# Ten of the 22 k rows of an FFN down projection by Strassen's seven products

## The chip, the cores and the metric

The kernel runs on one core of a Trainium2 chip. The metric is the device time of one execution in microseconds (us); the time given is the median of several runs. A profile of one further execution shows what each engine did: TensorE (PE, its weight loads apart as PEld), VectorE (DVE), ScalarE (ACT), GpSimd (POOL), and SyncE (SP), whose queue issues all the transfers here.

## The reference

Two layers of a bidirectional encoder on 512 tokens of width 1024. Each layer has four mixers (two kinds of attention over heads, a pooling mixer, and a latent attention), an output projection with a residual and a LayerNorm, and then a gated MLP with a short convolution. The change is in the last step of the MLP, the product with `w_down` (2816 x 1024):

```python
def _conv_ffn(x, w_up, conv_w, conv_b, w_down):
    u = x @ w_up
    u = lax.conv_general_dilated(u, conv_w[:, None, :], ...) + conv_b
    gate, up = jnp.split(u, 2, axis=-1)
    return (jax.nn.silu(gate) * up) @ w_down

def reference(...):
    for l in range(DEPTH):
        ...
        f = _conv_ffn(x, ffn_w_up[l], ffn_conv_w[l], ffn_conv_b[l], ffn_w_down[l])
        x = _layer_norm(DN_ALPHA * x + f, ln2_g[l], ln2_b[l])
    return x
```

## The kernel before

All matrix products are made in split precision: an operand x is held as hi = x rounded to the matmul's format and lo = x - hi, and a product is three matmuls, hi hi, hi lo and lo hi, summed in one PSUM bank (`mm3`). `hi_lo` makes the two parts: ACT casts (hi), then DVE subtracts (lo).

The kernel writes its instructions in an order that a planner chooses when the program is built. Each piece of work is a generator that says what it needs next (data, a free buffer, a PSUM bank); the planner follows expected times and gives every engine its fixed queue. On the chip each engine runs its queue in order and waits on semaphores. Two processes feed the weights: `p_raw` loads a group of weights (128 partitions x 1024 float32, 512 KB) through SP into a buffer of the pool "B" (34 buffers of 4 KB per partition), up to `DEPTH_RAW` = 4 groups ahead, and `p_split` makes hi and lo of it, up to `W.ahead` groups ahead of the group that TensorE uses.

A layer's MLP has two stages. In the up projection (`up_mm`), for each of 22 chunks of 128 channels (a "k row" of the next product), TensorE makes a gate half and an up half, 24 matmuls of 512 columns each; `up_post` adds the convolution (one ACT instruction, two on DVE), applies silu, multiplies gate and up on DVE, and splits the result into the tile G[j] (hi and lo, 128 x 512 each).

The down projection then has 22 k rows x 4 token tiles of 128 x 2 halves of 512 output columns. It is two calls of `gemm`. The first makes columns 0 to 511: 11 groups of two k rows, for each group 4 token tiles x 2 k rows x 3 matmuls into 4 PSUM banks, which hold the sums to the end of the call. `p_half` then adds each bank to the row of the residual (x times ALPHA) and takes statistics. The second call makes columns 512 to 1023 in the same way, with its last four groups done token tile by token tile (`tail`), so that the LayerNorm (`p_norm`) of one tile runs under the matmuls of the next.

Of the kernel before, what the change touches and what calls it, by code (L numbers as in the profile page):

```python
# [17 lines left out]
D = 1024  # L18
# [17 lines left out]
TAIL = 4  # L36
# [7 lines left out]
NB_E = 11  # L44
P_FIN, P_PREP, P_PV, P_T, P_S, P_G = 2, 1, 3, 4, 5, 9

# [52 lines left out]
    # -- memory  # L99
# [17 lines left out]
    # -- time  # L117
# [31 lines left out]
    # -- engines  # L149
# [71 lines left out]
    # -- processes  # L221
# [71 lines left out]
def trunk(ctx: ExitStack, tc: tile.TileContext, x_nat, x_t, pos, freqs, ident_d, bias_d, edge_d, ones_d,  # L293
# [35 lines left out]
    def hi_lo(hi, lo, src, scale=None, done=None):  # L329
        """steps: hi = f32r(src * scale), lo = src * scale - hi"""  # L330
# [18 lines left out]
    # ---------------- weights: loads run ahead, then raw -> (hi, lo)  # L349
    plan = []  # L350
    for l in range(DEPTH):
        plan += [(w_d[l, g], 832) for g in range(4)]
        plan += [(w_ab[l, c, g], 1024) for c in range(3) for g in range(4)]
        plan += [(w_c[l, c], 1024) for c in range(2)]
        plan += [(w_out[l, h, g], 1024) for h in range(2) for g in range(4)]
        plan += [(w_up[l, s * NCH + j], 1024) for j in range(NCH) for s in range(2)]
        plan += [(w_down[l, h, g], 1024) for h in range(2) for g in range(NCH // 2)]

    class W:
        raw, hl = {}, {}  # L360
        split, used, ahead, reserve, hold = 0, 0, AHEAD, RESERVE, False

    def p_raw():
        for n, (src, w) in enumerate(plan):
# [7 lines left out]
            P.dma(r[:, :w], src)  # L372
            W.raw[n] = r

    def p_split():
        for n, (src, w) in enumerate(plan):
            if n == 0:
                continue
            yield "if", lambda: n <= W.used + (min(URGENT, W.ahead) if W.hold else W.ahead) and n in W.raw
            yield "slot", "B", 2, lambda: max(0, W.reserve - 2)  # L380
# [17 lines left out]
    def drop(n):  # L398
        P.release(*W.hl.pop(n))

    # ---------------- constants
# [28 lines left out]
    def load_x(n):  # L430
        """the rows 256 n to 256 n + 256 of x^T, and before the second of them the first weights"""
# [157 lines left out]
    def gemm512(evac):  # L589
        """512 columns, some token tiles at a time"""  # L590
# [49 lines left out]
    def p_half(key, t, ps, cs, early=False):  # L640
        """x * alpha + ps for some columns of a row, and their statistics; early: a first part of ps alone"""
# [3 lines left out]
        if n < 512:  # L645
# [63 lines left out]
    def p_end(row, mv, rs, g, b, dst):  # L709
        """the last rows, in pieces: the output leaves as they are done"""  # L710
# [25 lines left out]
    # ---------------- one layer  # L736
    def layer(l, xkey):
# [32 lines left out]
        # ---- evacuations  # L770
# [16 lines left out]
        def evac_v(t, ps):  # L787
            """the values of A and of B"""
# [13 lines left out]
        def done_with(key):  # L802
            """one of the two that use the natural queries and keys is through with them"""
# [4 lines left out]
        # ---- D  # L808
# [89 lines left out]
        # ---- C  # L898
# [60 lines left out]
        # ---- queries and keys of a head  # L959
# [24 lines left out]
        def p_split_a(u):  # L984
            """[h h l] of the negated and scaled queries and [h l h] of the keys, side by side"""
# [29 lines left out]
        def stack_q(ps, dst, _, tok):  # L1015
            """a head's hi rows where they stand, its lo rows on the other 64 partitions"""
# [9 lines left out]
        def stack_k(ps, dst, kl, tok):  # L1026
            """a head's hi rows twice, and its lo rows twice"""
# [15 lines left out]
        def p_prep(kind, h):  # L1043
            u, h2 = h // 2, h % 2
            if kind == "B" and h2:
                QK[kind, h] = QK[kind, h - 1]
# [36 lines left out]
        # ---- attention  # L1083
# [171 lines left out]
        # ---- the stream of GEMMs  # L1255
        def stream():
# [40 lines left out]
            # gated MLP  # L1297
            G = [None] * NCH

# [17 lines left out]
            def up_post(j, side, keep):  # L1317
# [16 lines left out]
                yield "op", [(l, "silu", j), t1]  # L1334
                P.tt(t1, keep["t", 0], t1, ALU.mult)
# [21 lines left out]
            x2 = out if last else dr.tile([128, NT, D], F32, name=f"x2_{l}")  # L1357

            def LG(k):
                if k == NCH - 4:  # L1360
                    prog[0] = max(prog[0], 1)
                return G[k][:, 0], G[k][:, 1]

            def needg(k, t):
                return [(l, "G", k)]

            nk2 = (l, "x2")
            yield from gemm(512, LG, NCH, needg, lambda t, ps: P.spawn(p_half(k2, t, ps, slice(0, 512))))

            def after(g):  # L1370
                P.release(G[2 * g], G[2 * g + 1])
                if g >= 2:
                    prog[0] = 2
                if g >= 4:
                    W.ahead = 4

            yield from gemm(512, LG, NCH, needg, lambda *a: p_rest(k2, nk2, x2, last, *a), tail=TAIL, halve=True,
                            after=after)
            P.release(*G[-2 * TAIL:])
# [115 lines left out]
```

## Time and profile before

| | |
|---|---|
| median of 3 runs | 1224.42 us (1224.24 to 1224.9) |
| profiled execution, from first to last instruction | 1223.1 us (the page gives no other time of it) |
| TensorE busy | 1205.0 us, 6132 matmuls |
| VectorE busy | 804.0 us, 1305 instructions |
| ScalarE busy | 587.5 us, 1032 instructions |
| moved by DMA | 122.24 MB |

Busy times are sums over the span, and the stages differ much from one another. TensorE's clock is shown as the share granted: 1.00 is 2.4 GHz, 0.5 is 1.2 GHz.

### The profile page before, as it was taken

What the parts mean: (1) busy time and instruction counts of PE and PEld (TensorE: products, weight loads), DVE (VectorE), ACT (ScalarE), POOL (GpSimd) and SP (SyncE); (2) the same over time, 40 slices, a digit from 0 to 9 for tenths busy, and PEclk for the clock granted to TensorE, in tenths of its full rate; (3) what the DMA queues carried; (4) which work ended last, traced back from release to release, by engine and by line L of the source; (5) the groups of instructions that cost most, each with busy time, mean ns of one, the idle gap of its engine ahead of it and who ended that gap; (6) DMA issues with size and microseconds to landing.
All of it is one profiled execution on the core that took longest, in us unless ns stands there. A gap on an engine that the chain in (4) does not pass through costs nothing.

```text
span 1223.1 us, 16077 instructions
## 1 busy us (share of the span) xinstructions
PE 1205.0 (99%) x6132; PEld 1023.1 (84%) x6132; DVE 804.0 (66%) x1305; ACT 587.5 (48%) x1032; POOL 130.5 (11%) x247
## 2 busy tenths in 40 slices
PE   8999999999999999999999999999999999999997
PEld 7888888898888888888898888888988888888885
DVE  6678899875666666314656799989666666662325
ACT  6678787243444444212256878862444444441120
POOL 1320152100000000000131303501000000000002
PEclk9999999999999999999999999999999999999998
DMA  8112113371322222236351121234522322213431
GB/s 304 61 36 70 56 36 130 114 253 55 104 70 85 86 69 69 86 121 215 106 169 36 35 70 57 79 112 155 173 85 71 103 72 84 69 54 110 137 130 69
DMA packets 36221, 122.24 MB, mean 100 GB/s; under 512 B 5168, under 2 KB 6448, under 8 KB 36144
## 3 DMA queue, kind: packets, MB, share of 16 engines
q1 hardware_dynamic: 36144, 121.22, 30.5%
q8 instruction: 48, 0.79, 0.3%
q14 instruction: 29, 0.24, 0.1%
HBM read 112.81 MB, written 8.39 MB: 99 GB/s over the span
## 4 chain that ended last, share of the span: by engine, by line
PE 95%; DVE 3%; ACT 1%; issue 1%; POOL 0%; DMA 0%; POOLq 0%; DVEq 0%; ACTq 0%
PE ps_f L203 39%; PE g L203 29%; PE h L203 10%; PE ps_s L203 4%; PE ps_o L203 4%; PE ps_p L211 3%; PE ps_u L203 2%; PE ps_t L211 1%; PE ps_x L211 1%; PE ps_q L203 1%; PE ps_kv L203 0%; DVE m L199 0%; PE ps_r L211 0%; DVE lo L175 0%; DVE ptl L175 0%
## 5 line engine op out<-in xcount | busy, mean ns | idle before, releaser
L175 DVE TENSOR_TENSOR lo<-raw,hi 128x1024 fp32r<-128x1024 f32 (+2 forms) x185 | 223.8, 1218 | 179.0 <-ACT hi L167 156.4
L203 PE MATMUL ps_f<-xh,hi 128*128 128x512 f32 (+1 forms) x768 | 285.5, 372 | 0.0
L203 PE MATMUL ps_f<-xl,hi 128*128 128x512 f32 (+1 forms) x768 | 285.2, 371 | 0.0
L203 PE MATMUL ps_f<-xh,lo 128*128 128x512 f32 (+1 forms) x768 | 285.2, 371 | 0.0
L167 ACT CAST hi<-raw 128x1024 fp32r<-128x1024 f32 (+2 forms) x185 | 189.2, 1036 | 140.2 <-PE g L203 113.1
L203 PE MATMUL g<-hi,G 128*128 128x512 f32 (+1 forms) x712 | 217.9, 387 | 0.0
L183 DVE SCALAR_TENSOR_TENSOR t<-ps_f,cw,t 128x511 f32<-128x511 f32 x176 | 132.0, 750 | 74.7 <-ACT t L169 71.5
L203 PEld LDWEIGHTS ps_f<-xl,hi 128*128 128x128 f32 x768 | 144.7, 188 | 25.0
L203 PEld LDWEIGHTS ps_f<-xh,lo 128*128 128x128 f32 x768 | 144.6, 188 | 24.9
L203 PEld LDWEIGHTS ps_f<-xh,hi 128*128 128x128 f32 x768 | 144.7, 188 | 24.8
L203 PEld LDWEIGHTS g<-hi,G 128*128 128x128 f32 x712 | 133.3, 188 | 27.1
L203 PE MATMUL g<-lo,G 128*128 128x512 f32 (+1 forms) x356 | 137.6, 387 | 0.0
L169 ACT ACTIVATE t<-ps_f,cb,cw 128x512 f32<-128x512 f32 x88 | 68.5, 778 | 102.3 <-PE ps_f L203 102.3
L190 POOL TENSOR_SCALAR ve<-mv 128x1 f32<-128x1 f32 x16 | 10.7, 672 | 783.8 <-DVE mv L199 783.8
L203 PE MATMUL g<-hi,M 128*128 128x512 f32 (+1 forms) x264 | 87.0, 391 | 1.6 <-DVE m L199 1.6
L203 PE MATMUL h<-hi,xh 128*128 128x512 f32 x192 | 78.9, 411 | 0.0
L203 PEld LDWEIGHTS g<-lo,G 128*128 128x128 f32 x356 | 66.9, 188 | 13.6
L169 ACT ACTIVATE e<-ps_s,m 128x512 f32<-128x512 f32 x96 | 66.0, 690 | 21.9 <-DVE m L199 21.6
L203 PE MATMUL h<-hi,xl 128*128 128x512 f32 x192 | 75.3, 392 | 0.0
L203 PE MATMUL h<-lo,xh 128*128 128x512 f32 x192 | 75.3, 392 | 0.0
L167 ACT CAST G<-t 128x512 fp32r<-128x512 f32 x44 | 27.3, 621 | 99.5 <-DVE t L175 99.5
L199 DVE TENSOR_REDUCE m<-ps_s 128x1 f32<-128x512 f32 x96 | 63.3, 683 | 9.9 <-PE ps_s L203 9.0
(182 smaller groups left out, 1708.2 us busy)
## 6 DMA issues: line engine op xcount, KB each, us to landing
raw<-in_w_up SPq DMA_DIRECT2D x88, 512.0 KB, 3.5
raw<-in_w_down SPq DMA_DIRECT2D x44, 512.0 KB, 3.5
raw<-in_w_ab SPq DMA_DIRECT2D x24, 512.0 KB, 4.2
raw<-in_w_out SPq DMA_DIRECT2D x16, 512.0 KB, 3.6
x<-row SPq DMA_DIRECT2D x12, 512.0 KB, 6.3
row<-x SPq DMA_DIRECT2D x12, 512.0 KB, 4.2
raw<-in_w_d SPq DMA_DIRECT2D x7, 416.0 KB, 4.0
raw<-in_w_c SPq DMA_DIRECT2D x4, 512.0 KB, 3.3
```

The source lines that it names most:

```text
L167: self.nc.scalar.copy(out, in_)
L169: self.nc.scalar.activation(out, in_, func, **kw)
L175: self.nc.vector.tensor_tensor(out=out, in0=in0, in1=in1, op=op)
L183: self.nc.vector.scalar_tensor_tensor(out=out, in0=in0, scalar=scalar, in1=in1, op0=op0, op1=op1)
L190: e.tensor_scalar(out=out, in0=in0, scalar1=s1, op0=op0, **kw)
L199: fn(*a, **k)
L203: self.nc.tensor.matmul(out, lhsT, rhs, start=start, stop=stop)
L211: self.nc.tensor.transpose(out, in_, ident)
```

## The change

Of the 22 k rows of the down projection, 10 are now multiplied by Strassen's scheme, in five pairs (`NP` = 5). For a pair p the tokens are cut in two halves, the two k rows are the halves of the inner dimension, and the columns are cut in two halves, so that A (tokens x k) and B (k x columns) are 2 x 2 blocks. Seven products of sums of blocks take the place of eight, each of 2 token tiles x 3 matmuls per pair, and all ten rows' share of both column halves is made this way. The seven products are done in three sweeps over the five pairs: sweep a (three products, with A11+A22, A21+A22, A11+A12 against B11+B22, B11, B22), sweep b (two: A11 and A22-side differences against B12-B22 and B11+B12), and sweep c (two, against B21+B22 and B21-B11). The other 12 k rows' six groups for the first 512 columns (marked s) stand between the sweeps, in the order of `DOWN`: a0 a1 a2 a3 a4 s5 s6 b0 b1 b2 s7 b3 b4 s8 c0 c1 c2 s9 c3 c4 s10. After that the second `gemm` makes the last 512 columns of the 12 other rows, six groups with the same tail of four.

All sums are DVE instructions: in the up projection `up_post` leaves a pair's gated products in float32 (`GF`) and forms five sums of 128 x 256; the hi and lo parts of the seven left factors are made per sweep (`prep`, tiles `sA`, `sB`, at most `G_AHEAD` = 2 ahead); the weights' sums are made in `split_sums` (one of 128 x 512 for a group of sweep a, two for one of b or c) and then split, at most `S_AHEAD` = 3 ahead. From the third group on, split weights of the sweeps are kept in the four quarters of the tiles `xh` and `xl`, which held the up projection's input. A group of b or c is loaded in three transfers of 256 KB instead of one of 512 KB, one of a in two. `acc` adds each finished product bank into the rows of the residual: 12 additions of 128 x 512 for each of the two token tiles of a half.

The core of the diff (it also removes comments, and one added line in `p_prep` only waits for a dictionary entry):

```diff
+NP = 5
+S_FIRST = 2
+S_AHEAD = 3
+G_AHEAD = 2
 P_FIN, P_PREP, P_PV, P_T, P_S, P_G = 2, 1, 3, 4, 5, 9
+def down_order():
+    order = [("a", p) for p in range(NP)]
+    rest = [("s", g) for g in range(NP, NCH // 2)]
+    order += rest[:S_FIRST]
+    rest = rest[S_FIRST:]
+    n, m = 2 * NP, len(rest)
+    for i, e in enumerate([("b", p) for p in range(NP)] + [("c", p) for p in range(NP)]):
+        order.append(e)
+        while rest and (m - len(rest) + 1) * n <= (i + 1) * m:
+            order.append(rest.pop(0))
+    return order
+DOWN = down_order()
...
-        plan += [(w_down[l, h, g], 1024) for h in range(2) for g in range(NCH // 2)]
+        plan += [((l, s, p), 0) if s in "abc" else (w_down[l, 0, p], 1024) for s, p in DOWN]
+        plan += [(w_down[l, 1, g], 1024) for g in range(NP, NCH // 2)]
...
+            l, s, p = src
+            b11, b21 = (w_down[l, 0, p][:, c] for c in (slice(0, 512), slice(512, 1024)))
+            b12, b22 = (w_down[l, 1, p][:, c] for c in (slice(0, 512), slice(512, 1024)))
+            P.dma(r[:, 0:512], {"a": b11, "b": b12, "c": b21}[s])
+            P.dma(r[:, 512:1024], b22)
+            e = None
+            if s != "a":
+                e = etile("b11")
+                P.dma(e, b11)
+            W.raw[n] = (r, e)
...
+            W.inx[n] = q = W.freex.pop(0)
+            hi, lo = (x[:, 2 * q:2 * q + 2].rearrange("p k s -> p (k s)") for x in (XH, XL))
...
+            P.tt(e, raw[:, left], raw[:, right], ALU.add)
...
+            P.spawn(hi_lo(both[:, 0], both[:, 1], e, done=lambda: done(e)))
+            P.spawn(hi_lo(hi, lo, raw, done=lambda: done(raw)))
...
+        if s == "b":
+            P.tt(raw[:, right], raw[:, left], raw[:, right], ALU.subtract)
+            yield "op", [raw]
+            P.tt(raw[:, left], raw[:, left], e, ALU.add)
+        else:
+            P.tt(raw[:, right], raw[:, left], raw[:, right], ALU.add)
+            yield "op", [raw]
+            P.tt(raw[:, left], raw[:, left], e, ALU.subtract)
...
+        if (key, "started") in S:
+            yield "op", [ps, (key, "acc", t, cs.start // 512)] + ([(key, "early")] if n < 512 else [])
+            P.tt(row, row, ps[:, :n], ALU.add)
...
+            def acc(ps, parts):
+                yield "op", [key]
+                rows = S[key][0]
+                yield "op", [ps]
+                for t, half, op in parts:
+                    row = rows[t][:, 512 * half:512 * half + 512]
+                    if (t, half) not in left:
+                        left[t, half] = {(0, 0): 4, (0, 1): 2, (1, 0): 2, (1, 1): 4}[t // 2, half]
+                        assert op == ALU.add
+                        P.stt(row, row, ALPHA, ps, ALU.mult, ALU.add)
+                    else:
+                        P.stt(row, ps, 1.0 if op == ALU.add else -1.0, row, ALU.mult, ALU.add)
+                    left[t, half] -= 1
+                    if left[t, half] == 0:
+                        P.mark((key, "acc", t, half), rows[t])
+                P.release(ps)
...
+            for i, (s, p) in enumerate(order):
+                P.spawn(prep(i, s, p))
+            prog[0] = 1
+            S[key, "started"] = True
+            W.ahead = S_AHEAD
+            W.freex[:] = range(4)
+            plus, minus = ALU.add, ALU.subtract
+            where = {"a": [(0, [(0, 0, plus), (1, 1, plus)]), (1, [(1, 0, plus), (1, 1, minus)]),
+                           (None, [(0, 0, minus), (0, 1, plus)])],
+                     "b": [(0, [(0, 1, plus), (1, 1, plus)]), (1, [(1, 1, plus)])],
+                     "c": [(1, [(0, 0, plus), (1, 0, plus)]), (0, [(0, 0, plus)])]}
...
+                if j < 2 * NP:
+                    q = j // 2
+                    if j % 2 == 0:
+                        yield "slot", "B", 2
+                        GF[q] = [slot(f"GF{q}{i}", [128, 4, 256], F32) for i in range(2)]
+                    yield "if", lambda: q in GF
+                    su, ga = GF[q]
+                    P.tt(ga[:, 2 * (j % 2):2 * (j % 2) + 2], *(t.rearrange("p (a n) -> p a n", a=2)
+                                                               for t in (keep["t", 0], t1)), ALU.mult)
+                    P.release(keep["t", 0], t1)
+                    P.mark((l, "g", j), ga)
+                    if j % 2 == 0:
+                        return
+                    yield "op", [(l, "g", j - 1), (l, "g", j)]
+                    for d, x, y in ((0, 0, 3), (1, 1, 3), (2, 0, 2)):
+                        P.tt(su[:, d], ga[:, x], ga[:, y], ALU.add)
+                    P.mark((l, "GF", q, "a"), su)
+                    for d, y in ((1, 0), (2, 3)):
+                        P.tt(ga[:, d], ga[:, d], ga[:, y], ALU.subtract)
+                    P.mark((l, "GF", q), ga)
...
-            yield from gemm(512, LG, NCH, needg, lambda t, ps: P.spawn(p_half(k2, t, ps, slice(0, 512))))
...
+            yield from strassen(k2, G, GF, prog)
...
+            nk_ = NCH - 2 * NP
+            tail = min(TAIL, nk_ // 2)
+            prog[0] = 2
+            W.ahead = 4
```

Outside the two down projections the queues hold the same instructions in nearly the same order, and in both layers the rows of the down projection stand alike. On PE, the first rows of the down projection of layer 0 were these (g are the PSUM banks, one for each token tile; the moving operand is the weights' hi or lo, the stationary one the tile G):

```order
L203 MATMUL g_4807<-hi_4691,G_3297 128x512 [waits Activation_49]
L203 MATMUL g_4807<-lo_4692,G_3297 128x512 [waits DVE_49]
L203 MATMUL g_4807<-hi_4691,G_3297 128x512
L203 MATMUL g_4807<-hi_4691,G_3342 128x512
L203 MATMUL g_4807<-lo_4692,G_3342 128x512
L203 MATMUL g_4807<-hi_4691,G_3342 128x512
L203 MATMUL g_4817<-hi_4691,G_3297 128x512
```

They are now these (ma are the banks of sweep a's products, sum the split B11+B22, sA the split sums of the left factors):

```order
L224 MATMUL ma_4840<-sum_4701,sA 128x512 [waits Activation_49]
L224 MATMUL ma_4840<-sum_4701,sA 128x512 [waits DVE_49] x2
L224 MATMUL ma_4847<-sum_4701,sA 128x512 x3
L224 MATMUL ma_4854<-hi_4699,sA 128x512
L224 MATMUL ma_4854<-lo_4700,sA 128x512
...
L224 MATMUL ma_4864<-hi_4699,sB 128x512 [waits Activation_49]
L224 MATMUL ma_4864<-lo_4700,sB 128x512
L224 MATMUL ma_4864<-hi_4699,sB 128x512 [waits DVE_49]
...
L224 MATMUL ma_4840<-sum_4743,sA 128x512 [waits Activation_49]
L224 MATMUL ma_4840<-sum_4743,sA 128x512
L224 MATMUL ma_4840<-sum_4743,sA 128x512 [waits DVE_49]
```

A bank takes three matmuls of a group where it took six, and a group of sweep a has 18 matmuls where a group had 24; what a bank needs of ACT and DVE has grown from the weights' two parts to those of the sums on both sides.

On DVE, between two weights of the down projection there was nothing but the next weights' lo part until the first half's rows were added (row, st):

```order
L175 TENSOR_TENSOR lo_5023<-raw_4990,hi_5022 128x1024 [waits DMAHW0_49,PE_49,Activation_49]
L175 TENSOR_TENSOR lo_5053<-raw_5020,hi_5052 128x1024 [waits DMAHW1_49,PE_49,Activation_49]
L175 TENSOR_TENSOR lo_5083<-raw_5050,hi_5082 128x1024 [waits DMAHW2_49,PE_49,Activation_49]
L183 SCALAR_TENSOR_TENSOR row_5110<-row_5110,g_4807 128x512 [waits DMAHW4_49,DVE_49,PE_49]
L199 BN_STATS st<-row_5110 128x6 [waits DVE_49]
```

Now, before TensorE can begin b0 and b1, DVE's queue holds these rows (raw and b are the weights' blocks and their sums in place, xl the lo part of b0's weights, and then of b1's, row the residual's rows, to which the products of sweep a are added):

```order
L196 TENSOR_TENSOR sA<-GF_3557,sA 128x512 [waits Activation_49]
L196 TENSOR_TENSOR raw_4923<-raw_4923 128x512 [waits DMAHW7_49,DMAHW6_49]
L204 SCALAR_TENSOR_TENSOR row_4874<-ma_4864,row_4874 128x512 [waits PE_49]
L204 SCALAR_TENSOR_TENSOR row_4874<-row_4874,ma_4864 128x512
L204 SCALAR_TENSOR_TENSOR row_4875<-ma_4870,row_4875 128x512 [waits PE_49]
L204 SCALAR_TENSOR_TENSOR row_4875<-row_4875,ma_4870 128x512
L196 TENSOR_TENSOR raw_4923<-raw_4923,b_4926 128x512 [waits DMAHW0_49,DVE_49]
L196 TENSOR_TENSOR raw_5014<-raw_5014 128x512 [waits DMAHW2_49,DMAHW1_49]
L196 TENSOR_TENSOR raw_5014<-raw_5014,b_5017 128x512 [waits DMAHW3_49,DVE_49]
L196 TENSOR_TENSOR xl<-raw_4923,xh 128x1024 [waits Activation_49]
L196 TENSOR_TENSOR raw_5019<-raw_5019 128x512 [waits DMAHW5_49,DMAHW4_49]
L196 TENSOR_TENSOR xl<-raw_5014,xh 128x1024 [waits Activation_49]
```

Where one subtraction stood per group there are two sums, the subtraction and the left factor's, and four additions of products stand ahead of the sums for b0.

And between sweeps b and c, the last additions of b's products (mb) with the weights of c0, c1 and c2 behind them:

```order
L204 SCALAR_TENSOR_TENSOR row_4877<-mb_5113,row_4877 128x512
L204 SCALAR_TENSOR_TENSOR row_4876<-mb_5118,row_4876 128x512 [waits DVE_49,PE_49]
L196 TENSOR_TENSOR xl<-raw_5138,xh 128x1024 [waits Activation_49]
L204 SCALAR_TENSOR_TENSOR row_4877<-mb_5122,row_4877 128x512 [waits DVE_49,PE_49]
L196 TENSOR_TENSOR sA<-GF_3557,sA 128x512 [waits Activation_49]
L196 TENSOR_TENSOR raw_5149<-raw_5149 128x512 [waits DMAHW3_49,DMAHW2_49]
L196 TENSOR_TENSOR raw_5149<-raw_5149,b_5152 128x512 [waits DMAHW4_49,DVE_49]
L196 TENSOR_TENSOR raw_5182<-raw_5182 128x512 [waits DMAHW6_49,DMAHW5_49]
L196 TENSOR_TENSOR raw_5182<-raw_5182,b_5185 128x512 [waits DMAHW7_49,DVE_49]
L196 TENSOR_TENSOR xl<-raw_5149,xh 128x1024 [waits Activation_49]
L196 TENSOR_TENSOR lo_5305<-raw_5212,hi_5304 128x1024 [waits DMAHW0_49,Activation_49]
L196 TENSOR_TENSOR xl<-raw_5182,xh 128x1024 [waits Activation_49]
```

The additions wait for TensorE's last group of sweep b, and three weight groups that sweep c needs stand behind them in the queue.

## Rows read from the trace of the kernel before

**Rows 1.** The page: the span, and each engine's busy time (share, instructions).

```profile
span 1223.1 us, 16077 instructions
...
PE 1205.0 (99%) x6132; PEld 1023.1 (84%) x6132; DVE 804.0 (66%) x1305; ACT 587.5 (48%) x1032; POOL 130.5 (11%) x247
```

**Rows 2.** Windows: from:to, us, each engine's busy time, granted clock, DMA share, GB/s.

```profile
255.00:490.00 235.00, 235.00 (x1108) 197.56 (x1107) 146.92 (x174) 100.39 (x129) 0.00 (x0) 1.00 0.29 92
490.00:545.00 55.00, 55.00 (x244) 45.57 (x243) 13.91 (x13) 11.23 (x12) 0.00 (x0) 1.00 0.34 105
545.00:599.00 54.00, 54.00 (x241) 44.67 (x241) 25.94 (x31) 13.35 (x14) 1.71 (x2) 1.00 0.51 168
599.00:632.00 33.00, 33.00 (x186) 30.69 (x185) 20.64 (x34) 10.87 (x32) 8.14 (x15) 1.00 0.45 150
```

**Rows 3.** The chain that ended last, in order of time: start, us, what.

```profile
490.12 108.80 PE g L203 x480
```

**Rows 4.** Waits of PE: waited for; us in total, times, longest.

```profile
PE g L203 <- ACT hi L167: 5.0, 1, 5.0
...
PE g L203 <- DVE m L199: 1.6, 2, 0.8
```

**Rows 5.** Timeline of PE in the up projection: start, us; first and last of 19.

```profile
299.79 0.39 PE L203 MATMUL ps_f<-xl,hi 128*128 128x512 f32 x1
...
303.87 0.39 PE L203 MATMUL ps_f<-xl,hi 128*128 128x512 f32 x1
```

**Rows 6.** DVE by form: count | busy us, mean ns | idle before, releaser.

```profile
L175 DVE TENSOR_TENSOR lo<-raw,hi 128x1024 fp32r<-128x1024 f32 x176 | 215.7, 1233 | 172.0 <-ACT hi L167 152.4 <-PE g L203 17.0 <-DMA raw<-in_w_up 1.7
L183 DVE SCALAR_TENSOR_TENSOR t<-ps_f,cw,t 128x511 f32<-128x511 f32 x176 | 132.0, 750 | 74.7 <-ACT t L169 71.5
...
L175 DVE TENSOR_TENSOR t<-t,t 128x512 f32<-128x512 f32 x44 | 30.5, 692 | 1.5
L175 DVE TENSOR_TENSOR G<-t,G 128x512 fp32r<-128x512 f32 x44 | 30.4, 692 | 28.8 <-ACT G L167 28.8
...
L183 DVE SCALAR_TENSOR_TENSOR row<-row,g 128x512 f32<-128x512 f32 x32 | 21.8, 681 | 41.4 <-PE g L203 41.4
...
L175 DVE TENSOR_TENSOR sA<-qkA,sA 128x256 fp32r<-128x256 f32 x8 | 3.0, 412 | 0.0
```

**Rows 7.** ACT by form, same columns.

```profile
L167 ACT CAST hi<-raw 128x1024 fp32r<-128x1024 f32 x176 | 182.1, 1047 | 132.8 <-PE g L203 107.7 <-DMA raw<-in_w_down 18.8 <-DVE lo L175 5.5
L169 ACT ACTIVATE t<-ps_f,cb,cw 128x512 f32<-128x512 f32 x88 | 68.5, 778 | 102.3 <-PE ps_f L203 102.3
...
L169 ACT ACTIVATE t<-t 128x512 f32<-128x512 f32 x44 | 27.8, 632 | 68.8 <-DVE t L183 68.8
L167 ACT CAST G<-t 128x512 fp32r<-128x512 f32 x44 | 27.3, 621 | 99.5 <-DVE t L175 99.5
...
L167 ACT CAST sA<-qkA 128x256 fp32r<-128x256 f32 x8 | 2.8, 399 | 0.0
```

**Rows 8.** Timeline of DVE in the LayerNorm after layer 0's MLP: start, us.

```profile
593.52 0.69 DVE L183 SCALAR_TENSOR_TENSOR row<-row,g 128x512 f32<-128x512 f32 x1 [2.51 <-PE g L203]
594.24 0.69 DVE L199 BATCH_NORM_STATS2 st<-row 128x6 f32<-128x512 f32 x1
...
599.69 0.69 DVE L199 BATCH_NORM_STATS2 st<-row 128x6 f32<-128x512 f32 x1
600.30 0.68 DVE L175 TENSOR_TENSOR xl<-ps_x,xh 128x512 fp32r<-128x512 f32 x1
600.89 0.20 DVE L199 BATCH_NORM_AGGREGATE mv<-st 128x2 f32<-128x12 f32 x1
```

**Rows 9.** Transfers by line: count, KB each, median us to landing.

```profile
raw<-in_w_down SPq DMA_DIRECT2D x44, 512.0 KB, 3.5
...
xraw<-in_x_t SPq DMA_DIRECT2D x2, 256.0 KB, 3.5
```

**Rows 10.** Windows: the stretch with the busiest DMA.

```profile
10.00:15.00 5.00, 5.00 (x24) 4.89 (x24) 4.66 (x5) 4.27 (x6) 0.00 (x0) 1.00 1.03 417
```

More of the change, by code (lines that the diff above doesn't have):

```diff
@@ L371, in p_raw @@
             r = slot(f"raw{n}", [128, 1024], F32)
-            P.dma(r[:, :w], src)
-            W.raw[n] = r
+            if not w and src[1] != "a":
+                yield "slot", "e", 1, 4
+            if w:
+                P.dma(r[:, :w], src)
+                W.raw[n] = r
+                continue
+            l, s, p = src
+            b11, b21 = (w_down[l, 0, p][:, c] for c in (slice(0, 512), slice(512, 1024)))
+            b12, b22 = (w_down[l, 1, p][:, c] for c in (slice(0, 512), slice(512, 1024)))
@@ new lines, in p_raw, with split_sums, done @@
+            P.dma(r[:, 0:512], {"a": b11, "b": b12, "c": b21}[s])
[5 more added lines that the diff above has]
+            W.raw[n] = (r, e)
+    def split_sums(n, src):
+        s = src[1]
+        far = s != "a" or src[2] >= 2
+        if far:
+            yield "if", lambda: W.freex
+        if far:
+            W.inx[n] = q = W.freex.pop(0)
+            hi, lo = (x[:, 2 * q:2 * q + 2].rearrange("p k s -> p (k s)") for x in (XH, XL))
+        else:
+            yield "slot", "B", 2, lambda: max(0, W.reserve - 2)
+            hi, lo = slot(f"hi{n}", [128, 1024]), slot(f"lo{n}", [128, 1024])
+        if s == "a":
+            yield "slot", "B", 1
+            both = slot(f"sum{n}", [128, 2, 512])
+            yield "slot", "e", 1, 2
+            esum = etile("b12")
+        raw, e = W.raw.pop(n)
+        left, right = slice(0, 512), slice(512, 1024)
+        W.split += 1
+        if s == "a":
+            e = esum
+            W.hl[n] = (hi, lo, both)
+            yield "op", [raw]
+            P.tt(e, raw[:, left], raw[:, right], ALU.add)
+            got = []
+            def done(t):
+                P.release(t)
+                got.append(t)
+                if len(got) == 2:
+                    P.mark(("w", n), both, *tiles)
+            tiles = (hi, lo)
+            P.spawn(hi_lo(both[:, 0], both[:, 1], e, done=lambda: done(e)))
+            P.spawn(hi_lo(hi, lo, raw, done=lambda: done(raw)))
+            return
+        W.hl[n] = (hi, lo)
+        yield "op", [raw, e]
+        if s == "b":
[4 more added lines that the diff above has]
+            P.tt(raw[:, right], raw[:, left], raw[:, right], ALU.add)
+            yield "op", [raw]
+            P.tt(raw[:, left], raw[:, left], e, ALU.subtract)
+        P.release(e)
+        def done():
+            P.release(raw)
+            P.mark(("w", n), hi, lo)
+        P.spawn(hi_lo(hi, lo, raw, done=done))
@@ L379, in p_split @@
             yield "if", lambda: n <= W.used + (min(URGENT, W.ahead) if W.hold else W.ahead) and n in W.raw
+            if not w:
+                yield from split_sums(n, src)
+                continue
             yield "slot", "B", 2, lambda: max(0, W.reserve - 2)
@@ L1045, in p_prep @@
             if kind == "B" and h2:
+                yield "if", lambda: (kind, h - 1) in QK
                 QK[kind, h] = QK[kind, h - 1]
@@ L1357, in stream @@
             x2 = out if last else dr.tile([128, NT, D], F32, name=f"x2_{l}")
+            nk2 = (l, "x2")
+            yield from strassen(k2, G, GF, prog)
             def LG(k):
-                if k == NCH - 4:
-                    prog[0] = max(prog[0], 1)
-                return G[k][:, 0], G[k][:, 1]
+                return G[2 * NP + k][:, 0], G[2 * NP + k][:, 1]
             def needg(k, t):
-                return [(l, "G", k)]
-            nk2 = (l, "x2")
-            yield from gemm(512, LG, NCH, needg, lambda t, ps: P.spawn(p_half(k2, t, ps, slice(0, 512))))
-            def after(g):
[L1371 to L1377, printed above, removed]
+                return [(l, "G", 2 * NP + k)]
+            nk_ = NCH - 2 * NP
+            tail = min(TAIL, nk_ // 2)
+            prog[0] = 2
+            W.ahead = 4
+            def after(g):
+                P.release(G[2 * NP + 2 * g], G[2 * NP + 2 * g + 1])
+            yield from gemm(512, LG, nk_, needg, lambda *a: p_rest(k2, nk2, x2, last, *a), tail=tail, halve=True,
                             after=after)
-            P.release(*G[-2 * TAIL:])
+            P.release(*G[-2 * tail:])
             W.ahead = 4
```

82 lines of the change are left out of this document (79 added, 3 removed).

## The prediction

> **What bounds the kernel now.** I read the page first: TensorE is busy for 1205.0 of 1223.1 us, VectorE for 804.0 and ScalarE for 587.5 [rows 1]. A share of 99% asks for the windows, to see whether that holds in the stage that is changed. It does: in the down projection of layer 0 (490 to 599 us) PE is busy in every microsecond at a granted clock of 1.00 (2.4 GHz), while DVE is busy for 13.91 of 55 and 25.94 of 54 us, and DMA engines for half or less [rows 2]. The chain of waits agrees: 108.80 us of it are one unbroken piece of 480 matmuls into g [rows 3], and the longest wait of PE for ACT or DVE in such rows is the 5.0 us at the start, the rest 1.6 us in total [rows 4]. So each matmul taken away there shortens the kernel by its own step, and each wait put in its place lengthens it. The question is whether DVE, which is to make all the sums, keeps ahead of PE.
>
> **TensorE: the gain.** A product of two blocks takes 2 token tiles x 3 matmuls for a pair; eight products were 48 matmuls, seven are 42, five pairs make 240 into 210 for a layer, so 60 fewer in both, all of 512 columns. A step is (303.87 - 299.79)/18 = 0.2267 us in the up projection, where a bank takes 24 matmuls in a row [rows 5], and 108.80/480 = 0.2267 us in the down projection, where it takes six [rows 3]. A change of bank therefore costs nothing that can be seen, and I take the same step for banks that take three. Gain: 60 x 0.2267 = 13.6 us. No other matmul is added or removed, and the queues of the rest of the kernel stay nearly the same.
>
> The Trainium skill ("TensorE: Matmul & The Clock Gate", section "Wait — 56ns, not 53.3ns?") gives 215.7 ns from start to start for 512 columns at 2.4 GHz; by it the gain would be 12.9 us. The trace differs, at 226.7 ns, and the sum goes by the trace.
>
> **VectorE: the cost.** Counted from the queues of both layers: 48 additions of a product bank to a row of the residual, less 16 old ones that become plain additions; 86 more 128x512 operations (weight sums, left factors, those plain additions, less 20 lo parts of G); 10 more 128x1024 and 60 more 128x256. No row shows an addition of two float32 blocks in place; the nearest is t<-t,t at 0.692 us, bounded below by 0.59 (the start-to-start of two that don't depend on each other: 600.30 to 600.89 [rows 8]) and above by 0.750 (t<-ps_f). An addition of a bank is as row<-row,g, 0.681, or at most 0.750; 1.233 for 128x1024 and 0.412 for 128x256 [rows 6]. I take the middle ones, which have the same shapes and operands: 32 x 0.681 + 86 x 0.692 + 10 x 1.233 + 60 x 0.412 = 118.3 us. DVE goes from 804 to some 922 us, which is 76% of the span; but it falls in few stages.
>
> In the up projection it is hidden: a layer gains 25 sums x 0.412 and loses 10 lo parts x 0.692, +3.4 us, where DVE was busy for 146.92 of 235 us [rows 2]. ACT loses casts there; in all it gains 20 x 0.621 + 10 x 1.047 + 10 x 0.399 = 26.9 us [rows 7] and stays far behind DVE.
>
> In the sweeps it is not obviously hidden. DVE against PE for one group: sweep a, 3 x 0.692 + 1.233 + 0.412 = 3.72 against 18 x 0.2267 = 4.08 us; sweeps b and c, 3 x 0.692 + 1.233 = 3.31 against 12 x 0.2267 = 2.72; s, 1.233 against 5.44. With 24 additions of banks: 18.6 + 33.1 + 7.4 + 16.3 = 75.4 us against PE's 354 x 0.2267 = 80.25. That is 94% (before: 39.85 of 109), and b and c alone lag behind. The order of the rows decides, so I walk it, with T the end of the up projection on PE.
>
> The start: the gate half of the last chunk ends 24 steps before T, T-5.44. Behind it come ACT 0.778, two DVE rows of 0.750, silu 0.632 and the casts for sA 0.621 and sB 0.399, then their lo parts; with some 0.04 us for each hand-over the second ends at T-0.6. a0 can start at T; no wait.
>
> To b0: from T-0.6 DVE has 42 rows before the weights of b0 are split: 18 x 0.692, 6 x 1.233, 4 x 0.412, 2 x 0.750 and 12 additions x 0.681 = 31.2 us, so T+30.6. PE gets there after sweep a and two s, (90 + 48) x 0.2267 = T+31.3. Margin 0.7 us. The additions wait for nothing: the first bank is finished three steps into a4, at (72 + 3) x 0.2267 = T+17.0, and DVE reaches it, behind the first 24 of the 42, at T+17.8.
>
> To b2: six more rows, 5.8 us, T+36.4; PE T+36.7. Margin 0.3 us. b3 and b4 have s7 ahead of them, 5.44 us more.
>
> Between b and c: the first bank of b is finished three steps into b4, at 213 x 0.2267 = T+48.3; behind that stand 13 rows up to the weights of c1, 6 x 0.681 + 2 x 1.233 + 5 x 0.692 = 10.0 us, T+58.3; PE comes to c1 after 258 steps, T+58.5. Margin 0.2 us; c2, 2.5 us later, T+60.8 against T+61.2. Later groups have s9 and s10 ahead of them.
>
> Behind the sweeps, c4's first bank is finished at T+72.8, and three subtractions ahead of its additions end at about T+73.5; then come 6 x 0.681 + 4 x 0.692 + 3 x 1.233 us and five statistics of at most 0.69 [rows 8], 14.0 us, up to the last weights of the tail, T+87.5. PE wants these after two more groups and three token tiles' worth of the tail, 80.25 + 10.88 + 4.08 = T+95.2. The end is as before.
>
> These margins use whole durations. Two DVE rows that don't depend on each other start 0.59 to 0.61 us apart though each lasts 0.68 or 0.69 [rows 8]; most of the 42 rows are of that kind, and 25 x 0.08 = 2.0 us more margin results (an estimate). So the likeliest sum has no wait: span 1223.1 - 13.6 = 1209.5. The median of the runs stood 1.3 us above the span, and I keep that: **1210.8 us**.
>
> **The loads.** A group of b or c comes in three transfers of 256 KB, four groups ahead (`DEPTH_RAW`), that is some 11 us or more; w_down's 512 KB landed in 3.5 us, and so did 256 KB of xraw [rows 9]. I cost them at nothing; the bounds are in the last rival.
>
> **Rivals.** A: DVE's instructions don't overlap, and each pays a hand-over of 0.03 us besides its duration (594.24 - 593.52 - 0.69 [rows 8], where the second needs the first). Then b0 is ready at 30.6 + 42 x 0.03 = T+31.9, 0.6 us late, b2 another 0.5, c1 another 0.2: 1.3 us a layer, 2.6 in all, 1213.4 us. For it: many of the new rows are pairs that depend on each other. Against: the starts of 600.30 and 600.89.
>
> The Trainium skill says that the next operation of VectorE cannot issue until the pipe is empty ("VectorE: DVE Perf Modes", section "The DRAIN you can't avoid"), which speaks for A, though it names exceptions; the starts at 600.30 and 600.89 don't agree with it.
>
> B: the new forms are slower than their neighbours, by the 8% that lie between 0.692 and 0.750. Then b0 is 31.2 x 0.08 - 0.7 = 1.8 us late, b2 0.8 more, c1 0.6 more: 3.2 us a layer, 6.5 in all, 1217.3 us. For it: nothing but that no row shows them. Against: PSUM and SBUF operands, sums and differences, all lie between 0.681 and 0.692 here.
>
> C, on the other side: the loads bound sweeps b and c. Ten groups of 768 KB and four of 512 KB are 9.96 MB in the 49 us from b0 to the end of s10, 203 GB/s, where the down projection had 105 and 168 [rows 2]. Slower than before from 6.8 us of waits a layer, that is below 9.96 MB/55.8 us = 179 GB/s. For it: 256 KB took as long to land as 512 KB. Against: 168 GB/s took a share of only 0.51 (330 at a full share), and 417 were reached [rows 10]. If the short runs halved the 330, the stretch would take 60.4 us, 11.4 more, and the kernel 1233.6 us.
>
> **Chances.** No wait worth counting 0.70 (1209.6 to 1212), A 0.15, B 0.11, C 0.04. What a measurement can tell is about 0.2%, 2.4 us; the first three are faster by more: 0.95 with a little kept for a wait that I don't see, same 0.01, slower 0.04. The range reaches from 1209.6 over A and halfway to B: 1216.0.
>
> **What would show it.** Right: 60 matmuls fewer at the same step, PE busy near 1191 us, no gap at b0, b2, c1 above some tenths, DVE near 922 us and busy for over nine tenths of the 80 us behind T, DMA 10.5 MB more. Wrong: gaps of PE on xl of the weights of b0, b2 or c1 (A, B), with DVE's forms at 0.75 (B); DVE or ACT waiting for raw or b in the sweeps (C); a step other than 0.2267 on ma, mb, mc.

## The result, and the profile after

The changed kernel takes 1211.43 us (median of four runs, 1211.25 to 1211.76), against 1224.44 us of the kernel before on the same chip: a ratio of 0.9895, with a 95% interval of 0.9881 to 0.9909. The profiled execution has a span of 1210.0 us. The prediction was 1210.8 us.

The page after, span and busy times, answers to [rows 1]:

```profile
span 1210.0 us, 16328 instructions
PE 1192.3 (99%) x6072; PEld 1012.0 (84%) x6072; DVE 902.8 (75%) x1493; ACT 609.9 (50%) x1072; POOL 131.3 (11%) x247
```

There are sixty matmuls fewer, and PE's busy time is lower by 12.7 us; the span is lower by 13.1. DVE has 188 instructions more, as many as were counted, and its busy time rose by 98.8 us without lengthening the span.

Windows (from:to, us; busy time of PE, PEld, DVE, ACT and POOL; granted clock, DMA share, GB/s) of the sweeps in layer 0 and in layer 1; they answer to the second and third row of [rows 2]:

```profile
490.00:570.00 80.00, 80.00 (x354) 66.10 (x353) 71.04 (x97) 34.97 (x45) 0.00 (x0) 1.00 0.68 228
1080.00:1160.00 80.00, 80.00 (x354) 66.10 (x353) 69.45 (x95) 37.70 (x51) 0.00 (x0) 1.00 0.64 213
```

PE is busy in every microsecond of both, at a granted clock of 1.00 (2.4 GHz). DVE is busy for 71.04 and 69.45 of 80 us, so 8.96 us are left in layer 0's sweeps. The experiments come back to that idle time.

The chain of waits in the down projection of layer 0 (start, us, what) answers to [rows 3]:

```profile
490.23 20.52 PE ma L224 x90
510.75 10.91 PE g L224 x48
521.66 8.16 PE mb L224 x36
529.82 5.44 PE g L224 x24
535.26 5.44 PE mb L224 x24
540.70 5.44 PE g L224 x24
546.14 8.16 PE mc L224 x36
554.30 5.44 PE g L224 x24
559.74 5.44 PE mc L224 x24
565.18 27.20 PE g L224 x120
```

The one piece of 480 matmuls has become ten, each beginning where the one ahead ends. Divide any of them by its count: 0.2267 us for a matmul, in ma, mb and mc as in g, but for 0.12 us in the piece of 90 (0.19 in layer 1). So the sweeps hold no gap.

The waits of PE (waited for; us in total, times, longest) answer to [rows 4]. No tile of the sweeps is among the larger ones:

```profile
PE g L224 <- ACT hi L188: 4.9, 1, 4.9
PE g L224 <- DVE m L220: 1.6, 2, 0.8
```

How late DVE runs is read from its timeline (start, us) at the weights of the first and third b group and of the second c group, their last step being xl, beside PE's first matmul of the sweeps and the first that reads the xl of b0, b2 and c1, each the second matmul of its group:

```profile
490.07 1.52 PE L224 MATMUL ma<-sum,sA 128*128 128x512 f32 x6
...
521.72 0.39 PE L224 MATMUL mb<-xl,sA 128*128 128x512 f32 x1
...
527.16 0.39 PE L224 MATMUL mb<-xl,sA 128*128 128x512 f32 x1
...
548.92 0.39 PE L224 MATMUL mc<-xl,sA 128*128 128x512 f32 x1
```

```profile
507.35 3.08 DVE L204 SCALAR_TENSOR_TENSOR row<-row,ma 128x512 f32<-128x512 f32 x5 [1.30 <-PE ma L224]
...
516.33 0.69 DVE L196 TENSOR_TENSOR raw<-raw 128x512 f32<-128x512 f32 x1
517.05 0.69 DVE L196 TENSOR_TENSOR raw<-raw,b 128x512 f32<-128x512 f32 x1
517.66 1.22 DVE L196 TENSOR_TENSOR xl<-raw,xh 128x1024 fp32r<-128x1024 f32 x1
...
523.49 1.22 DVE L196 TENSOR_TENSOR xl<-raw,xh 128x1024 fp32r<-128x1024 f32 x1
...
538.69 3.09 DVE L204 SCALAR_TENSOR_TENSOR row<-mb,row 128x512 f32<-128x512 f32 x5 [3.17 <-PE mb L224]
...
546.68 1.22 DVE L196 TENSOR_TENSOR xl<-raw,xh 128x1024 fp32r<-128x1024 f32 x1
```

With T = 490.07, b0 is ready at 518.88, T+28.8. PE starts its group one step of 0.23 us ahead of the row at 521.72, at T+31.4: a margin of 2.6 us. b2 is ready at T+34.6 against T+36.9 (2.2), c1 at T+57.8 against T+58.6 (0.8). The texts of the experiments have 2.5, 2.1 and 0.7, since they take PE's times from the prediction. Five additions of a bank take 3.08 us together, so they start 0.60 us apart; the pair 516.33 and 517.05, where the second needs the first, starts 0.72 apart.

The Trainium skill ("VectorE: DVE Perf Modes", section "The DRAIN you can't avoid") says of an operation of VectorE that a next one that is not held back starts before the pipe is empty. The trace agrees for independent additions, 0.60 us apart at 0.68 each.

### The profile page after: what moved, and what is told of

Its sections match the earlier page's. It is cut to its first block, busy times and chain, and to the rows that moved or that the text cites. A ratio compares the mean times of both kernels' runs of the same rounds, so it can differ in the third digit from the quotient of the medians.

```text
span 1210.0 us, 16328 instructions
## 1 busy us (share of the span) xinstructions
PE 1192.3 (99%) x6072; PEld 1012.0 (84%) x6072; DVE 902.8 (75%) x1493; ACT 609.9 (50%) x1072; POOL 131.3 (11%) x247
## 2 busy tenths in 40 slices
DMA packets 44864, 132.75 MB, mean 110 GB/s; under 512 B 6129, under 2 KB 7409, under 8 KB 44785
## 4 chain that ended last, share of the span: by engine, by line
PE 95%; DVE 3%; ACT 1%; issue 0%; POOL 0%; DMA 0%; SPq 0%; POOLq 0%; DVEq 0%; ACTq 0%
PE ps_f L224 40%; PE g L224 21%; PE h L224 10%; PE ps_s L224 4%; PE ps_o L224 4%; PE ma L224 3%; PE ps_p L232 3%; PE mc L224 2%; PE mb L224 2%; PE ps_u L224 2%; PE ps_t L232 1%; PE ps_x L232 1%; PE ps_q L224 1%; PE ps_kv L224 0%; DVE m L220 0%
## 5 line engine op out<-in xcount | busy, mean ns | idle before, releaser
L196 DVE TENSOR_TENSOR lo<-raw,hi 128x1024 fp32r<-128x1024 f32 (+2 forms) x169 | 203.5, 1217 | 76.9 <-ACT hi L188 69.5
L188 ACT CAST hi<-raw 128x1024 fp32r<-128x1024 f32 (+2 forms) x169 | 172.2, 1035 | 22.9 <-PE g L224 12.3
L224 PE MATMUL g<-hi,G 128*128 128x512 f32 (+1 forms) x392 | 120.7, 385 | 0.0
L224 PEld LDWEIGHTS g<-hi,G 128*128 128x128 f32 x392 | 73.2, 188 | 14.6
L224 PE MATMUL g<-lo,G 128*128 128x512 f32 (+1 forms) x196 | 75.4, 385 | 0.0
L196 DVE TENSOR_TENSOR ptl<-ps_p,pth 128x512 fp32r<-128x512 f32 x96 | 64.4, 680 | 1.6 <-ACT pth L188 1.0
L190 ACT ACTIVATE t<-t 128x512 f32<-128x512 f32 x44 | 27.9, 634 | 70.4 <-DVE t L204 70.4
```

What stands on the lines that cost most here:

```text
L188: self.nc.scalar.copy(out, in_)
L190: self.nc.scalar.activation(out, in_, func, **kw)
L196: self.nc.vector.tensor_tensor(out=out, in0=in0, in1=in1, op=op)
L224: self.nc.tensor.matmul(out, lhsT, rhs, start=start, stop=stop)
```

## The experiments

The theory is that of the prediction, called cover here: TensorE sets the time, each 512-column matmul removed is worth 0.2267 us, and VectorE's sums cost nothing as long as each group's weights are split before TensorE comes to it. The rivals: the sums cost time wherever they stand (each pays its whole duration), or their place doesn't matter, or the loads are the limit. Each experiment is an edit of the changed kernel, whose time is 1211.4 us.

**The undivided groups at the end.** `DOWN` is made a, b, c and only then the six groups s, so that nothing stands ahead of the sums:

```diff
-S_FIRST = 2
+S_FIRST = 0
...
-    for i, e in enumerate([("b", p) for p in range(NP)] + [("c", p) for p in range(NP)]):
-        order.append(e)
-        while rest and (m - len(rest) + 1) * n <= (i + 1) * m:
-            order.append(rest.pop(0))
-    return order
+    order += [("b", p) for p in range(NP)] + [("c", p) for p in range(NP)]
+    return order + rest
```

> The sweeps a, b, c run one behind the other, and the six groups s of the first columns come after them; the work and the counts are the same. Cover theory (the groups s between the sweeps give VectorE the time for its sums; independent rows of VectorE start 0.60 us apart): b0 waits behind 12 additions of banks, one sum and a subtraction that start when the first bank is done at T+17.0, 13 x 0.60 + 1.14 = 8.9 us, so 5.6 us of wait; b1 another 2.3, c0 2.1, c1 2.8; 12.8 us a layer, 25.6 in all, about 1237 us. Rival (VectorE's rows do not overlap and pay a hand-over, 0.72 each): about 15.5 us a layer, 1242 us. Rival (the place of s does not matter, since VectorE is far from bound): 1211.4 us.

Measured: 1238.22 us, ratio 1.0113 (1.0098 to 1.0128), slower than before the change. The waits of PE:

```profile
PE mb L221 <- DVE xl L193: 11.4, 3, 5.5
PE mc L221 <- DVE xl L193: 6.1, 4, 2.0
```

The stretch behind the longest wait, which ends at 515.75 us:

```profile
515.00:520.00 5.00, 4.25 (x12) 3.19 (x12) 4.96 (x8) 2.47 (x3) 0.00 (x0) 0.66 0.24 91
```

The same instructions in another order cost 26.8 us. 17.5 of them are these waits for the split weights, and 0.7 one for xh on ACT. The other 8.6 are PE's own busy time, 1200.9 us against 1192.3: behind the longest wait the granted clock was 0.66, so that a wait costs more than its own length. The place decides, as the cover theory said. But that its 1237 us came so close is in part luck. It counted 25.6 us of waits and nothing for the clock: the waits at b0 came as forecast (5.45 and 5.43 us against 5.6), those at b1 and c1 were shorter, and the clock made up the rest. The loads are not the cause: the chain of waits passes two of them in layer 1 and none in layer 0, and PE waits 5.4 us at b0 in both.

**The weights' sums left out.** The two additions per b and c group are dropped, so the products of b and c are made from the wrong blocks; everything else is done.

```diff
-            P.tt(raw[:, right], raw[:, left], raw[:, right], ALU.subtract)
-            yield "op", [raw]
-            P.tt(raw[:, left], raw[:, left], e, ALU.add)
+            pass
...
-            P.tt(raw[:, right], raw[:, left], raw[:, right], ALU.add)
-            yield "op", [raw]
-            P.tt(raw[:, left], raw[:, left], e, ALU.subtract)
+            pass
```

> Leaves out the two sums of weight blocks of every group of sweeps b and c (the blocks are split and multiplied as they were loaded); transfers, casts and matmuls stay. 40 x 0.69 us of VectorE's work go. Cover theory: PE waited for none of it, so the time stays within 0.5 us of 1211.4. Rival (the sums still cost the 0.6 us by which the gain fell short of 13.6 us): 1210.8 us or a little less.

Measured: 1211.29 us. DVE's busy time fell from 902.8 to 877.4 us, 0.64 us for each of 40 sums, and the kernel's time by 0.1, less than its runs differ among themselves. The sums are free where they stand.

**One and two more sums per group.** An addition of 128 x 512 that no result needs is put behind the two sums of each b and c group, ahead of its split, once or twice (`range(2)`):

```diff
+            for _ in range(1):
+                P.tt(e, raw[:, right], raw[:, right], ALU.add)
```

Two of them:

> Adds two more 128x512 additions on VectorE to every group of b and c (into a spare tile, results unused), 40 in all, 24 us of starts at 0.60. Cover theory with the margins read in the changed kernel's trace (b0 2.5 us, b2 2.1, c1 0.7, c2 1.1): b0 no wait, b2 1.5 us, c1 about 2 us; 3.5 a layer, about 1218 us. Rival (the margins of the prediction by whole durations, 0.7, 0.3 and 0.2 us): 4 x 0.72 - 0.7 = 2.2 at b0, 1.5 more at b2, 2.5 at c1; 6 a layer, about 1223.5 us. Rival (VectorE has room everywhere): 1211.4 us.

One, run later:

> One more 128x512 addition on VectorE for each b and c group, instead of two. Measured margins: with 0.60 to 0.72 us each, the three additions ahead of the third b group take 1.8 to 2.2 us of a margin of 2.1 us, the idle time ahead of the mb additions (3.2 us) takes up what the b groups added, and the two ahead of the second c group take 1.2 to 1.4 us of 0.66 us: a wait of about 0.6 us in each of the two sweeps, 1212.5 us. Rival (no threshold, each addition delays the tensor engine by its share of what two for each group cost): 1217.8 us. Rival (VectorE's idle time in the sweep, 13.9 us, takes up the 6 us wherever they stand): 1211.4 us.

(The idle time of 13.9 us in this text is a misreading of mine: 66.10 in the window is PEld's column. DVE's is 71.04, so it was idle for 8.96 us.)

Measured: 1211.99 us with one, 1224.20 (1222.14 to 1225.95 in ten runs) with two. The window of the sweeps in layer 0, first with one and then with two:

```profile
490.00:570.00 80.00, 80.00 (x354) 66.09 (x353) 77.05 (x108) 36.20 (x46) 0.00 (x0) 1.00 0.68 228
```

```profile
490.00:570.00 80.00, 75.57 (x331) 61.48 (x330) 77.98 (x109) 33.45 (x43) 0.00 (x0) 1.00 0.64 218
507.00:556.00 49.00, 44.57 (x194) 35.92 (x193) 48.45 (x69) 15.55 (x19) 0.00 (x0) 1.00 0.62 206
1158.75:1163.13 4.38, 4.38 (x12) 3.48 (x13) 4.31 (x7) 2.94 (x3) 0.00 (x0) 0.61 0.84 227
```

With one, DVE's busy time rises by 6.01 us, 0.60 for each of ten, and PE still has no gap. The wait of 0.6 us that I had expected at c1 did not come: the order on DVE was chosen anew, and in it c1's weights are ready at 546.43, 2.3 us before PE reads their xl at 548.70.

With two, DVE's busy time would be 83.1 of 80 us. DVE is busy for 48.45 of the 49 us between the a sweep's additions and the middle of c, and PE loses 4.43 us in the window, 8.9 us in both layers, all on xl. The 8.96 us of idle time lie between ten and twenty sums, so it says about how much more work fits; the place still decides whether it does, as the runs with six pairs show.

The time with two, 1224.20 us, is nearer to the rival with whole durations (1223.5) than to my 1218. But the rival's wait of 2.2 us at b0 is not there. In layer 0 PE waits 1.67 us at b2, 0.25 at c1 and 2.52 at c2, 4.4 us where I had 3.5. What I had left out is the clock: of the 10.9 us that the profiled execution lost, 8.9 are waits and 2.0 are PE's own busy time (1194.3 us against 1192.3). 1.9 of these stand in the last row above, behind a wait of 2.51 us at c2 of layer 1: eleven matmuls take 4.38 us instead of 2.49, at a granted clock of 0.61. The ten runs scatter by 3.8 us, and their clock goes with it: 0.997 in the mean of a run in the five of up to 1223.5 us, 0.995 or 0.996 in the five from 1224.9 us on.

**The loads two groups ahead instead of four**, for the groups of the sweeps (`w` is 0 for these):

```diff
-            yield "if", lambda: n < W.split + DEPTH_RAW
+            yield "if", lambda: n < W.split + (DEPTH_RAW if w else 2)
```

> The w_down halves of the a, b and c groups are loaded no more than two groups ahead of their sums, instead of four. If the loads have slack, as predicted: no change, 1211.4 us (within 0.6). If they are near their limit (the rival of the loads): each group waits for its transfers, 1214 us or more.

Measured: 1215.68 us (1215.33 to 1215.94), so the expectation of no change was wrong. But the b and c sweeps show no wait; PE's waits have one new row:

```profile
PE ma L224 <- ACT sA L188: 2.2, 2, 1.1
```

where it is, in PE's timeline, and ACT's timeline ahead of it:

```profile
491.02 2.00 PE L224 MATMUL ma<-sum,sA 128*128 128x512 f32 x6 [1.09 <-ACT sA L188]
```

```profile
487.51 1.03 ACT L188 CAST xh<-raw 128x1024 fp32r<-128x1024 f32 x1
489.83 0.62 ACT L188 CAST sum<-b 128x512 fp32r<-128x512 f32 x1 [1.29 <-DVE xl L196]
490.36 0.61 ACT L188 CAST sA<-GF 128x512 fp32r<-128x512 f32 x1
```

The loss is at T, once in each layer. The casts of the weights and of the left factors stand in one queue on ACT. In the changed kernel the cast of the first left factor, sA, comes first (488.09) and xh behind it (490.88). Here xh and sum of a group of weights stand ahead of sA, and sum waits 1.29 us for DVE's xl, so sA is late. No wait for a transfer stands ahead of T; ACT's only one in these 45 us, 0.8 us, ends at 499.96. So the shorter lead costs its time here through the order of ACT's queue, which was chosen anew, and not through a late transfer or the loads' rate: 228 GB/s were moved at a share of 0.68 in the changed kernel without a wait. Within the sweeps a lead of two groups is enough. Why the order came out so is not shown. The first six matmuls of ma take 2.00 us where they took 1.52, at a granted clock of 1.00: behind the first two PE waits for the lo part of sA, which DVE makes last. With twice that 0.5 us, and the 2.2 us of waits, some 3 us of the 4.2 have a place.

**Four pairs.** `NP = 4`, the rest by the same rule:

> Four pairs instead of five, the rest as in the changed kernel. Cover theory: no waits, and 12 matmuls more, 1211.4 + 2.7 = 1214.1 us. Rival (part of the gain with five pairs is lost in waits or costs that each pair brings, which the trace puts under other names): below 1213.3 us.

Measured: 1214.73 us (1214.06 to 1215.1), 3.3 us more than with five. Twelve matmuls are worth 2.7, and no new wait of PE appeared. So five pairs lose nothing that four would not.

**Six pairs.** `NP = 6`, the groups s still spread by the kernel's rule, which leaves three for the twelve b and c groups and puts none between b and c:

> Six pairs by Strassen in place of five (12 of the 22 k rows), five groups s left. 12 matmuls fewer, 2.7 us: 1208.7 us if VectorE still hides its sums. By start-to-start times it has 76.5 us of work in the 84.3 us of the sweeps (five pairs: 68.3 of 80.25). Cover theory: some waits at b and c, 0 to 1 us a layer, so 1208.7 to 1211. Rival (each of VectorE's rows takes its whole duration): 88 us of work in 84.3, more than 2 us of waits a layer, 1213 us or more.

Measured: 1217.51 us (1215.63 to 1217.87), a miss. The chain (start, us, what) at the seam of b and c:

```profile
541.50 3.41 PE mb L224 x15
...
544.93 1.35 DVE row L204 x3
...
551.55 1.15 DVE xl L196
552.70 0.04 issue
552.74 4.30 PE mc L224 x11
557.04 5.46 PE g L224 x24
```

At 544.9 DVE gets the additions of the mb banks and the sums of the first c groups together, and nothing stands on PE to cover them. In each layer PE waits 1.7 us on xl and twice some 0.2 us on row (a bank that isn't free). And then the eleven matmuls of mc take 4.30 us instead of 2.49. The window of these says why:

```profile
552.74:557.04 4.30, 4.30 (x12) 3.43 (x13) 4.26 (x7) 2.51 (x3) 0.00 (x0) 0.62 0.24 99
```

The granted clock is 0.62 over this stretch, behind an idle time of 1.67 us: it is 0.50 (1.2 GHz) to 555 us and 1.00 from 556. Waits of 4.2 us in both layers and 2 x 1.8 us of slower matmuls are 7.8 of the 8.6 us by which this span (1215.9) is longer than 1210.0 - 2.7. The rival's number (1213 or more, over 2 us of waits a layer) came, but not its reason: independent rows of DVE start 0.60 us apart here too, and the next run has the same work without these waits.

**Six pairs, the groups placed by hand**, one of them at that seam:

```diff
+    for piece in "ss", "bbb", "s", "bbb", "s", "ccc", "s", "ccc":
+        for s in piece:
+            order.append(rest.pop(0) if s == "s" else (s, sum(x[0] == s for x in order)))
```

> Six pairs instead of five, with the undivided rows' groups placed by hand: two after the a sweep, one after each three of the b and c groups, so that one of them stands between the last b and the first c group, where the run with six pairs waited. Cover theory (VectorE's sums are late only where too little undivided work stands ahead of them): no wait of the tensor engine in the sweeps, 12 matmuls of 0.2267 us fewer than with five pairs, 1211.4 - 2.7 = 1208.7 us. Rival (six pairs fill VectorE, and no order helps): 1214 us or more, with waits of more than 1 us in each sweep and VectorE busy through them.

Measured: 1209.69 us (1209.31 to 1209.87), ratio 0.9878 (0.9862 to 0.9895). This version beats the kernel before. Its four runs all lie below the four of the changed kernel, by 1.74 us in the median, and its span is 1208.0 us against 1210.0; but the intervals of the two ratios overlap, so its lead over the changed kernel is likely and not certain. The window with the even spread, then with the groups placed by hand, and the one new wait:

```profile
490.00:570.00 80.00, 77.85 (x333) 63.07 (x332) 71.43 (x98) 37.58 (x51) 0.00 (x0) 0.98 0.70 239
```

```profile
490.00:570.00 80.00, 80.00 (x354) 66.16 (x353) 71.64 (x98) 39.37 (x53) 0.00 (x0) 1.00 0.70 245
```

```profile
PE g L220 <- DVE row L200: 0.6, 2, 0.3
```

PE is busy throughout again with the same sums as in the run before, in another order: all three single groups have moved, not only the one that now stands at the seam. DVE is as busy (71.64 us) as where PE waited (71.43), so its idle time in the stretch alone does not decide. Of the 2.7 us for 12 matmuls 0.6 go to a wait for a bank behind the last c group, where the changed kernel has a group s and this one none.

**Seven pairs**, in the order `"ss", "bbbb", "s", "bbb", "s", "ccccccc"`:

> Seven pairs, with the four groups left placed by hand: two after the a sweep, one after the fourth b group, one between the last b and the first c group, and none among the seven c groups. Cover theory, with the distances of the run with six pairs in that order (the second to sixth c groups had their sums 5.9, 8.2, 13.0, 16.0 and 19.7 us after the end of the b sweep, about 3.7 us from one to the next; a seventh would have them at 23.4): the tensor engine comes to the sixth and seventh at 19.2 and 22.0, so it waits some 0.5 and 0.9 us, 1.4 in each sweep, which takes back the 2.7 us of 12 matmuls fewer: 1209.7 - 2.7 + 2.8 = 1209.8 us, no better than six. Rival (place and not amount of VectorE's work decides, and nothing waits): 1207.0 us. Rival (past six pairs VectorE is full): 1213 us or more.

Measured: 1225.37 us (1224.64 to 1227.3). Waits of PE:

```profile
PE mc L220 <- DVE xl L192: 4.4, 6, 0.8
PE ps_x L228 <- DVE row L200: 1.9, 1, 1.9
PE g L220 <- DVE row L200: 1.4, 2, 0.7
```

and behind the sweeps, first this run and then the changed kernel:

```profile
580.00:610.00 30.00, 27.39 (x135) 22.18 (x134) 29.52 (x46) 7.62 (x12) 3.85 (x6) 1.00 0.43 148
```

```profile
580.00:610.00 30.00, 30.00 (x156) 26.08 (x154) 22.94 (x38) 6.97 (x10) 5.13 (x8) 1.00 0.39 129
```

The waits among the c groups came, 2.2 us in a layer where I had 1.4. What I had not counted is that late sums push the additions of mc into the stretch of the LayerNorm, where DVE is now busy for 29.52 of 30 us: layer 0's down projection (first ma to the next layer's first h) took 140.0 us against 135.4, and the end from layer 1's first ma 125.7 against 122.1. Another 5.6 us went between layer 1's first h and its first ma, where the order of the queues was chosen anew. Waits of PE on S, KT and ptl (1.3, 1.2 and 0.7 us), which the changed kernel does not have, are 3.2 of them; the rest is open. So the rival "VectorE is full past six" has the better number, though the window of the sweeps does not show it full. Only this order of seven was run, so whether another would be faster is open too.

## Why the prediction was right

**TensorE's gain.** 60 x 0.2267 = 13.6 us was forecast, and the span fell by 13.1. 0.31 us of the difference are the two pieces of 90 matmuls above; the step in ma, mb, mc is 0.2267 elsewhere. With four pairs the same price holds within 0.6 us. The median came out 0.6 us above the forecast: 0.5 of it is this shortfall, and 0.1 that the median stands 1.4 us above the span where 1.3 was kept.

**VectorE's cost at nothing.** Right, and shown from both sides: without 40 of the sums the time is the same, with ten more per layer nearly so, and with twenty more, or without the s groups ahead of them, PE waits on xl as named in "what would show it". The one term that was mis-sized is DVE's busy time: 118.3 us more forecast, 98.8 measured. The count of 188 instructions was right, and so were the durations; three of the forms that no row of before had (count | busy us, mean ns | idle before, releaser), beside [rows 6]:

```profile
L196 DVE TENSOR_TENSOR sA<-GF,sA 128x512 fp32r<-128x512 f32 x30 | 20.4, 687 | 2.3 <-ACT sA L188 2.3
...
L196 DVE TENSOR_TENSOR raw<-raw,b 128x512 f32<-128x512 f32 x20 | 13.8, 691 | 0.5
...
L204 DVE SCALAR_TENSOR_TENSOR row<-mb,row 128x512 f32<-128x512 f32 x12 | 7.5, 685 | 6.3 <-PE mb L224 6.3
```

Count times mean, summed over all forms, rose by 118.7 us. But independent instructions overlap by 0.08 us, so that each occupies 0.60, and the page's busy time counts the overlap only once. With it one sign of being right was missed: DVE is busy for 71.04 of the 80 us behind T, 0.89 and not over nine tenths. PE's 1192.3 us and the 10.5 MB more of DMA (132.75 against 122.24) came as said. The estimate of 2.0 us more margin at b0 was of the right size: 2.6 against 0.7.

**The walk.** Right in its places and order, short in its margins: 2.6, 2.2 and 0.8 us where 0.7, 0.3 and 0.2 were forecast. As a guide to other edits such margins were worth less: the planner orders the queue anew for each, and one more sum per group, which should have overrun the margin at c1, brought no wait.

**The rivals.** A (each pays its hand-over, 1213.4) and B (new forms 8% slower, 1217.3) fall with the rows of the timeline: independent rows start 0.60 us apart, a hand-over is paid only where one needs the other (0.72), and no new form of 128 x 512 is above 0.692 us in the mean. C (the loads) falls as stated, since 213 to 228 GB/s were moved in the sweeps without a wait, where the change was to lose below 179. But the loads were not as free as "I cost them at nothing" says: with a shorter lead the kernel lost 4.2 us, some 3 of them at the entry to the sweeps by the order of ACT's queue. One sum is off: halfway from A (1213.4) to B (1217.3) is 1215.4 us, not 1216.0; the measured time is far below both.

## What to carry to other kernels

Work that moves from the bounding engine to a second one is free where the second has idle time in the same stretch and has the results ready before they are needed. Both are needed: with six pairs DVE was busy for 71.4 or 71.6 of 80 us, and PE waited in one order and not in the other. Measure that stretch, not the whole run, and count an independent instruction at its start-to-start distance (0.60 us here) rather than its duration (0.68). Then put work of the bounding engine that needs no sums where the sums come in a bunch, here at the seam between two sweeps: the same instructions took 1217.5 us by an even spread and 1209.7 with the three single groups placed by hand, one of them at the seam. And read a wait of TensorE with what follows it: behind 1.67 us of idle time eleven matmuls took 1.8 us longer here, at a lower clock.

## What the runs showed that was not expected

- Behind idle times of PE of 1.67 us (six pairs), 5.45 us (the groups at the end) and 2.51 us (two more sums per group, layer 1) the granted clock was 0.62, 0.66 and 0.61 in the windows shown. Behind 1.67, 2.52 and 1.68 us, with two more sums per group, it stayed at 1.00. So the length of an idle time alone does not decide, and these runs don't show what does.
- Loads held to two groups ahead cost 4.2 us without a wait for a transfer ahead of the sweeps; what changed there is the order of ACT's queue.
- The w_down transfers of 256 KB landed in 3.2 us (into raw) and 4.7 us (into b) in the median, no slower than those of 512 KB (5.2).
